# First quarter of the conv input projection summed in two halves of its contraction, its loads reordered, the norm's vector order written out, and the low parts of the expert rows made by TensorE

## Chip, cores and metric

One core of a Trainium2 chip runs one fused program. The metric is the device time of the whole program in microseconds (us), as the median of the runs shown. TensorE (PE) multiplies, VectorE (DVE) and ScalarE (ACT) work elementwise, GpSimd (POOL) does a few small steps, and SyncE (SP) issues the transfers of the weights.

## What is computed

The first block modulates a normed `x` by products of a condition vector (`ada`), runs a conformer convolution, and then a mixture of 32 experts with two chosen per token. A second block follows (latent attention and block attention), which the change does not touch.

```python
mod = silu(c) @ ada_w + ada_b                     # sh1, sc1, g1, sh2, sc2, g2
h = rmsnorm(x, norm_mix_g) * (1 + sc1) + sh1      # 256 tokens x 1024
u = h @ conv_w_in + conv_b_in;  a, gt = split(u)
u = a * sigmoid(gt)
y = depthwise_conv(u, w_dw, 31 taps) + b_dw
y = silu(layernorm(y) * ln_g + ln_b) @ conv_w_out
x = x + g1 * y
h = rmsnorm(x, norm_ffn_g) * (1 + sc2) + sh2
x = x + g2 * hier_moe(h)                          # group, top 2 of 8, 32 experts
...
```

## The kernel before, in words

**Weights.** `PIECES` lists all weights as pieces of about 2 MB. `W.fill` issues their loads on SyncE's queue in that order, each into one of six rotating buffers (later up to ten) as soon as the piece that used the buffer has been read; `W.get` hands the next one out. So the list sets the order in which weights land, and the end of the last reader of a buffer sets when a later load starts.

**Precision.** A product of the projections is made of three fp32r products: each operand is split into a high part (`wh`, `hh`, `yh`, `xh`; a ScalarE copy) and a low part (`wl`, `hl`, `yl`, `xl`; a VectorE subtraction), and high x high, low x high and high x low are summed.

**Head.** `x` is normed (`xn`) and turned (`pt`, copied to `xT`). `ada_cols` makes one 1024-vector of the modulation in two pieces: eight products `adp`, a ScalarE copy `ads`, four transposes `adc`, two short vector steps into `modc`. Vector 1 scales `xT`, vector 0 is added in `hh` (ScalarE) and `hl` (VectorE). Only when all eight 128-row chunks of `hh` and `hl` stand does the first of 16 sums `pu` begin: 24 products each, four sums for each quarter `cwi` of `conv_w_in`. The two sums of a channel group `m` are gated into `up`.

**Convolution.** VectorE runs 31 taps (L408, L411) for channel groups 0 to 3, TensorE (`pvv`, `py`) does groups 4 to 7. L479 subtracts a provisional mean.

**Norm and output.** `pms` and `pst` are column statistics, `rst` and `prs` spread the reciprocal deviation, L577 multiplies, L579 is the silu (`ysl`), and `po` multiplies by `conv_w_out`.

**Router and rows.** After the residual, VectorE runs some 35 short steps that choose the experts (up to `oh`, `pp`, `posp`), and ScalarE, GpSimd and VectorE make the scaled rows' high and low parts `xh2` and `xl2`, which the products `acc` gather for the first experts. Then 32 experts stream through `pgu` and `pys`.

A scheduler orders instructions on each engine, except where `keep_in_program_order` or a filled `pe_order` (for TensorE) holds the order of the text.

Of the kernel before, what the change touches and what calls it, by code (L numbers as in the profile page):

```python
# [13 lines left out]
P = 128  # L14
# [34 lines left out]
LN_DVE = ()  # L49
HALVED = (3,)  # L50
# [28 lines left out]
WARM_R = 2, 3  # L79
# [5 lines left out]
def pieces():  # L85
# [10 lines left out]
    add_ada(1)  # L96
    add_ada(0)
    for q in range(4):
        add((KD, 512), "cwi", 256 * q)
# [39 lines left out]
class Weights:  # L139


    def __init__(self, nc, pools, ahead):
        self.nc, self.pools, self.ahead = nc, pools, ahead
        self.src, self.tiles, self.nload, self.nget, self.cap = [], [], 0, 0, 1 << 30
        self.named, self.cuts = {}, {}
# [8 lines left out]
    def fill(self, upto):  # L154
        while self.nload < min(upto, self.cap, len(self.src)):
# [6 lines left out]
            if len(shape) == 2:  # L162
                v = v.rearrange("p (a b) -> p a b", a=shape[0])
            elif len(shape) == 3:
                v = v.rearrange("p (a b c) -> p a b c", a=shape[0], b=shape[1])
            h = n // self.cuts.get(self.nload, 1)
            for i in range(0, n, h):
                self.nc.sync.dma_start(t[:, i:i + h], ap[:, i:i + h])
            self.tiles.append(v)
# [16 lines left out]
def build(tc, A, out, dbg=None, stop=None):  # L186
# [53 lines left out]
    W.cuts = {**{i: 2 for i in HALVED}, MOE_TO - 1: LAST_CUT}  # L240
# [25 lines left out]
    crep = pre.tile([P, KD, 32], F32, name="crep")  # L266
    modc = const.tile([P, 48], F32, name="modc")
# [21 lines left out]
    def ada_part(psp, pool, ps=None):  # L289
        w = W.get()  # L290
        pt = psp.tile([P, 512], F32, name="adp", tag="adp")
        for k in range(KD):
            j = k % 4
            mm(pt[32 * j:32 * j + 32, :], crep[:, k, :], w[:, k, :], k < 4, k >= 4)
        if ps is None:
            ps = pool.tile([P, 512], F32, name="ads", tag="ads")
        nc.scalar.copy(ps, pt)
        return ps

    def ada_cols(v, psp, pool):  # L300
        for h in range(2):
            ps = ada_part(psp, pool)
            pc = psp.tile([P, 4, 4, 32], F32, name="adc", tag="adc")
            for q in range(4):
                nc.tensor.transpose(pc[:, q].rearrange("p j r -> p (j r)"), ps[:, P * q:P * q + P], ident)
            c = slice(8 * v + 4 * h, 8 * v + 4 * h + 4)
            nc.vector.reduce_sum(modc[:, c], pc[:, :, :, 0], axis=AX.X)
            nc.vector.tensor_add(modc[:, c], modc[:, c], vec[:, V_AB + 8 * v + 4 * h:V_AB + 8 * v + 4 * h + 4])
# [47 lines left out]
    def transpose_k(src, k):  # L356
        pt = psU.tile([P, T], F32, name="pt", tag="tp")
        for t in range(NT):
            nc.tensor.transpose(pt[:, P * t:P * t + P], src[:, t, P * k:P * k + P], ident)
        return pt  # L360

    ada_cols(1, psA, wk)
# [3 lines left out]
    nc.vector.scalar_tensor_tensor(aff[:, 0, :], modc[:, 8:16], 1.0, vec[:, V_MIX:V_MIX + 8],  # L366
                                   op0=OP.add, op1=OP.mult)
    for k in range(KD):
        nc.vector.tensor_scalar(xT[:, k, :], xT[:, k, :], aff[:, 0, k:k + 1], None, op0=OP.mult)
    def halves(w, c0):  # L370

        ws = []
        for i in range(2):
            wh = wsp.tile([P, 4, P], F32R, name="wh", tag="wh")
            wl = wsp.tile([P, 4, P], F32R, name="wl", tag="wl")
            split(wh, wl, w[:, 4 * i:4 * i + 4, c0:c0 + P])
            ws.append((wh, wl))
# [14 lines left out]
    def uproj(w, c0, ws=None):  # L392
        ws = ws or halves(w, c0)
# [42 lines left out]
    up = None  # L436
    for q in range(4):
        w = W.get()
        for i in range(2):
            m = 2 * q + i  # L440
            pg = uproj(w, P * i, first if m == 0 else None)
            pa = uproj(w, 256 + P * i)
            if up is None:
                up = xy.tile([P, KD, UW], F32, name="up", tag="up")
                nc.gpsimd.memset(up[:, :, 0:PADL], 0.0)
            sg = wk.tile([P, T], F32, name="sg", tag="sg")
            nc.scalar.activation(sg, pg, AF.Sigmoid, bias=vec[:, V_BIN + 8 + m:V_BIN + 9 + m])
            nc.vector.scalar_tensor_tensor(up[:, m, PADL:], pa, vec[:, V_BIN + m:V_BIN + m + 1], sg,
                                           op0=OP.add, op1=OP.mult)
    del w, first  # L450
# [67 lines left out]
    for group in CONV:  # L518
# [4 lines left out]
        for k in group:  # L523
# [27 lines left out]
    def rows_of(w, k):  # L551
# [3 lines left out]
        split(wh, wl, w[:, k, :])  # L555
        return wh, wl

    wo = W.peek(wo_at - W.nget)
    wos = [rows_of(wo, k) for k in range(WSP)]
    del wo  # L560

    nc.vector.tensor_copy(st[:, 0:4], pst)
    nc.vector.tensor_mul(st[:, 2:4], st[:, 2:4], st[:, 2:4])
    nc.vector.scalar_tensor_tensor(st[:, 0:2], st[:, 0:2], EPS, st[:, 2:4], op0=OP.add, op1=OP.subtract)
    nc.gpsimd.tensor_tensor(out=st[:, 0:2], in0=st[:, 0:2], in1=expn[:, 0:2], op=OP.pow)
    rst = wk.tile([P, T], F32, name="rst", tag="mp", bufs=1)
    for t in range(NT):
        nc.vector.tensor_scalar(rst[:, P * t:P * t + P], ident, st[:, t:t + 1], None, op0=OP.mult)
# [3 lines left out]
    for k in range(KD):  # L572
# [3 lines left out]
    for k in range(KD):  # L576
        nc.vector.tensor_mul(y[:, k, :], y[:, k, :], prs)  # L577
        ys = wk.tile([P, T], F32, name="ysl", tag="ht")
        nc.scalar.activation(ys, y[:, k, :], AF.Silu, scale=vec[:, V_LNG + k:V_LNG + k + 1],  # L579
                             bias=vec[:, V_LNB + k:V_LNB + k + 1])  # L580
        if k in LN_DVE:
            nc.vector.tensor_copy(yh[:, k, :], ys)
            nc.vector.tensor_sub(yl[:, k, :], ys, yh[:, k, :].bitcast(F32))
        else:
            split(yh[:, k, :], yl[:, k, :], ys)
# [93 lines left out]

    pw = psU.tile([P, 512], F32, name="pw", tag="pu")  # L680
    for i in range(WARM_R[0]):
        mm(pw, ident, g2b[:, 0:512], True, True)
# [1006 lines left out]
```

## Time and profile before

| | us |
|---|---|
| median of 3 runs | 946.4 (945.88 to 947.05) |
| the profiled execution | 945.95 |
| its span in the trace | 944.3 |
| TensorE busy in the span | 869.0 (92%) |
| VectorE busy | 526.6 (56%) |
| ScalarE busy | 361.2 (38%) |
| GpSimd busy | 58.2 (6%) |

The profiled execution spends 1.65 us outside the span, and lies 0.45 us under the median. The shares are averages over stages with different limits, so the rows further below are taken by stage.

### The profile page before, as it was taken

The page shows a single profiled execution, that of the slowest core. Times are in us where ns is not written, and L with a number is a line of the kernel's source. Part 1 is how long each engine was busy: PE and PEld are TensorE (multiplying, and loading weights), DVE is VectorE, ACT ScalarE, POOL GpSimd, SP SyncE. Part 2 cuts the span into 40 slices and gives each one's busy share as a digit, 9 for nine tenths or more (in the row PEclk, how much of TensorE's full clock was granted, in tenths as well). Part 3 has the DMA queues.
Part 4 walks back from the last instruction along what each step waited for, and adds up shares of the span by engine and source line. Part 5 has one row for each costly group of instructions (what it writes and reads, how often), then busy time and mean ns, then how long its engine had stood idle before and what let it go on. Part 6 is the DMA issues. An engine that isn't in the chain of part 4 may idle for free. (4 is left out here: it accounts for less than half of the span.)

```text
span 944.3 us, 15434 instructions
## 1 busy us (share of the span) xinstructions
PE 869.0 (92%) x6227; PEld 609.6 (65%) x6227; DVE 526.6 (56%) x1243; ACT 361.2 (38%) x788; POOL 58.2 (6%) x62
## 2 busy tenths in 40 slices
PE   4899879899999999999699999878999996999996
PEld 1597346665565555656356555538988874988975
DVE  2699965623343333334223342357777868758876
ACT  1455645412122121212012121145766735655761
POOL 0000210100000000000000000003100004110112
PEclk9899989999999999999899999999999998999998
DMA  9994968789999999999999999974432441624211
GB/s 372 411 389 191 406 249 317 323 362 426 427 427 428 426 427 426 427 426 430 422 428 425 426 429 425 425 311 159 170 140 91 179 178 45 255 102 179 90 45 45
DMA packets 23580, 289.44 MB, mean 307 GB/s; under 512 B 2736, under 2 KB 3408, under 8 KB 6096
## 3 DMA queue, kind: packets, MB, share of 16 engines
q1 hardware_dynamic: 21872, 282.29, 72.4%
q10 hardware_dynamic: 1632, 6.11, 1.8%
q8 instruction: 51, 0.84, 0.4%
q14 instruction: 25, 0.20, 0.1%
HBM read 287.34 MB, written 1.05 MB: 305 GB/s over the span
## 5 line engine op out<-in xcount | busy, mean ns | idle before, releaser
L197 PE MATMUL pgu<-w,xg 128*64 128x256 f32 x2048 | 233.5, 381 | 4.2 <-DMA w<-in_moe 4.2
L197 PEld LDWEIGHTS pgu<-w,xg 128*64 128x64 f32 x2048 | 145.6, 137 | 90.1 <-issue 20.8
L197 PE MATMUL pys<-w,hTe 128*64 128x512 f32 x512 | 116.1, 594 | 5.4 <-DMA w<-in_moe 2.5
L283 DVE TENSOR_TENSOR sl<-w,sh 128x1024 fp32r<-128x1024 f32 (+2 forms) x82 | 98.0, 1204 | 20.4 <-ACT sh L282 19.2
L282 ACT CAST sh<-w 128x1024 fp32r<-128x1024 f32 (+2 forms) x82 | 81.4, 1001 | 48.9 <-PE pj L197 46.0
L1012 DVE SCALAR_TENSOR_TENSOR yt<-pys,gs,g2b 64x512 f32<-64x512 f32 x64 | 48.0, 750 | 87.2 <-PE pys L197 86.2
L282 ACT CAST yh<-yt 64x512 fp32r<-64x512 f32 x64 | 39.6, 618 | 138.9 <-DVE yt L1012 137.3
L197 PE MATMUL pj<-xh,sh 128*128 128x256 f32 x304 | 86.6, 285 | 0.1
L197 PE MATMUL pj<-xl,sh 128*128 128x256 f32 x304 | 85.5, 281 | 0.0
L197 PE MATMUL pj<-xh,sl 128*128 128x256 f32 x304 | 85.3, 281 | 0.0
L197 PEld LDWEIGHTS pys<-w,hTe 128*64 128x64 f32 x512 | 36.2, 137 | 65.9 <-issue 54.5
L854 DVE TENSOR_TENSOR hid<-pgu,hid 128x256 f32<-128x256 f32 x32 | 13.6, 425 | 97.2 <-ACT hid L853 97.2
L853 ACT ACTIVATE hid<-pgu 128x256 f32<-128x256 f32 x32 | 12.3, 385 | 125.8 <-PE pgu L197 119.7
L197 PEld LDWEIGHTS pj<-xh,sh 128*128 128x128 f32 x304 | 57.1, 188 | 2.2 <-issue 1.6
L197 PEld LDWEIGHTS pj<-xl,sh 128*128 128x128 f32 x304 | 57.0, 188 | 1.8 <-issue 1.7
L197 PEld LDWEIGHTS pj<-xh,sl 128*128 128x128 f32 x304 | 57.1, 188 | 0.8 <-issue 0.8
L411 DVE SCALAR_TENSOR_TENSOR y<-up,wdw,y 128x256 f32<-128x256 f32 x120 | 54.9, 513 | 0.1
L283 DVE TENSOR_TENSOR yl<-yt,yh 64x512 fp32r<-64x512 f32 x64 | 44.0, 687 | 2.2 <-ACT yh L282 0.2
L197 PE MATMUL pu<-hh,wh 128*128 128x256 f32 x128 | 37.4, 292 | 2.7 <-ACT wh L282 2.7
L283 DVE TENSOR_TENSOR wl<-w,wh 128x512 fp32r<-128x512 f32 x48 | 33.2, 702 | 12.0 <-ACT wh L282 10.5
L282 ACT CAST wh<-w 128x512 fp32r<-128x512 f32 x48 | 29.3, 620 | 27.5 <-PE pu L197 20.4
L862 DVE COPY hTe<-pth 128x256 f32<-128x256 f32 x32 | 13.6, 425 | 44.6 <-PE pth L203 40.1
(343 smaller groups left out, 1579.2 us busy)
## 6 DMA issues: line engine op xcount, KB each, us to landing
w<-in_moe SPq DMA_DIRECT2D x95, 2048.0 KB, 32.0
w<-in_wst SPq DMA_DIRECT2D x32, 2048.0 KB, 8.7
w<-in_wst SPq DMA_DIRECT2D x5, 1152.0 KB, 5.1
w<-in_wst SPq DMA_DIRECT2D x2, 1536.0 KB, 11.2
wb<-in_wbd ACTq DMA_DIRECT2D x4, 512.0 KB, 7.0
w<-in_wst SPq DMA_DIRECT2D x2, 1024.0 KB, 22.6
w<-in_moe SPq DMA_DIRECT2D x4, 512.0 KB, 31.2
x<-in_x SPq DMA_DIRECT2D x1, 1024.0 KB, 11.5
```

The source lines that it names most:

```text
L197: ins = nc.tensor.matmul(o, l, r, start=start, stop=stop)
L282: a = nc.scalar.copy(hi, src)
L283: return a, (eng or nc.vector).tensor_sub(lo, src, hi.bitcast(F32))
L411: nc.vector.scalar_tensor_tensor(y[:, m, :], u, wdw[:, m, k:k + 1], y[:, m, :], op0=OP.mult, op1=OP.add)
L853: nc.scalar.activation(hid, pgu[:, 0:256], AF.Silu)
L854: nc.vector.tensor_mul(hid, pgu[:, 256:512], hid)
L862: nc.vector.tensor_copy(hT, pt.rearrange("p (q j s) -> p q j s", q=2, j=2))
L1012: nc.vector.scalar_tensor_tensor(yt[r, :], pys[r, :], gs[r, e % 2:e % 2 + 1], g2b[r, 512 * j:512 * j + 512], op0=OP.mult, op1=OP.mult)
```

## The change

1. **Loads.** `x` is loaded ahead of the weights. The list becomes: half 0 of modulation vectors 1 and 0, the first quarter `cwi` 0, then half 1 of vectors 1 and 0. The rows of `cwi` 0 that the second half of the sums needs (`LATE`) are loaded behind those.
2. **First quarter in halves.** Chunks 0 to 3 of `hh` and `hl` are made from the first halves of the modulation, and the four sums `pu` of the first quarter run over these chunks; chunks 4 to 7 follow. TensorE's order in the head is that of the text. Filler products `warm` (256 columns, their results unused) stand in it. Every second `xT` copy goes to ScalarE. The two sums beyond `psU`'s two buffers take `psA` tags.
3. **Norm.** ScalarE's and VectorE's order from the first `wo` splits to the last `yl` is written out; the second `adp` of the gate moves ahead of `prs`; the silu's table is loaded by an early dummy.
4. **Rows.** The low parts `xl2` of the rows are no longer made by GpSimd (row block 1) and VectorE (row block 0), but by TensorE: a product of `diag(rs2)` (`dr`) with `x2` in fp32, minus `xh2` by a negated identity, and a ScalarE copy out of PSUM. The filler products `pw` there go.

```diff
-LN_DVE = ()
-HALVED = (3,)
+LATE = {2: 4}
-WARM_R = 2, 3
+HEAD_WARM = (2, 1, 2, 1, 2)
...
-    add_ada(1)
-    add_ada(0)
-    for q in range(4):
+    for h in range(2):
+        for v in (1, 0):
+            add((KD, 512), "ada", v * D + h * 512)
+        if h == 0:
+            add((KD, 512), "cwi", 0)
+    for q in range(1, 4):
...
+            if self.nload in self.late:
+
+                self.rest[self.late[self.nload]] = t, ap
+                n //= 2
...
+    nc.sync.dma_start(x2, A["x"][0].rearrange("(t p) d -> p t d", p=P))
+    W.fill(3)
     nc.sync.dma_start(cstp, A["cst"][:, C_SEL:])
-    W.fill(1)
-    nc.sync.dma_start(x2, A["x"][0].rearrange("(t p) d -> p t d", p=P))
...
+    def ada_half(v, h, psp, pool, between=None):
+        ps = ada_part(psp, pool)
+        if between is not None:
+            between()
+        pc = psp.tile([P, 4, 4, 32], F32, name="adc", tag="adc")
+        for q in range(4):
+            tr(pc[:, q].rearrange("p j r -> p (j r)"), ps[:, P * q:P * q + P])
...
+    pe_order.append(1)
     xT = xy.tile([P, KD, T], F32, name="xT", tag="up")
     for k in range(KD):
-        nc.vector.tensor_copy(xT[:, k, :], transpose_k(xn, k))
...
+        (nc.scalar.copy if k % 2 else nc.vector.tensor_copy)(xT[:, k, :], transpose_k(xn, k))
...
+    def warm(n):
+
+        if n:
+            pw = psU.tile([P, T], F32, name="pw", tag="tp")
+            for i in range(n):
+                mm(pw, ident, x2[:, 0, 0:T], True, True)
...
+    def uproj_half(pu, i, wh, wl, between=None):
+        for k in range(4 * i, 4 * i + 4):
+            for n, (l, r) in enumerate(((wh, hh), (wh, hl), (wl, hh))):
+                mm(pu, l[:, k % 4, :], r[:, k, :], k == 0 and n == 0, k == KD - 1 and n == 2)
...
+    scale_half(0, HEAD_WARM[0])
+    shift_half(0, HEAD_WARM[1])
+    w = W.get()
+    quarter = [half(w, c0, 0) for c0 in (0, 256, P, 256 + P)]
+    warm(HEAD_WARM[2])
+    pus = [psU.tile([P, T], F32, name="pu", tag="pu") for i in range(2)]
+    pus += [psA.tile([P, T], F32, name="pu", tag=g) for g in ("adr", "pmu")]
+    for j in range(4):
+        uproj_half(pus[j], 0, *quarter[j])
+        if j == 2:
+            scale_half(1, 0)
+    warm(HEAD_WARM[3])
+    shift_half(1, HEAD_WARM[4])
+    warm(HEAD_WARM[4])
+    quarter = [half(w, c0, 1) for c0 in (0, 256, P, 256 + P)]
+    for j in range(4):
+        uproj_half(pus[j], 1, *quarter[j])
...
+    centre(0, 1, 2, 3, 4)
+    gate1.append(wk.tile([P, 512], F32, name="ads", tag="ads"))
+    keep(nc.scalar.copy(gate1[1], gate1.pop(0)))
+    keep(nc.scalar.activation(small[:, 8:9], small[:, 0:1], AF.Silu))
+    keep(nc.vector.tensor_copy(st[:, 0:4], pst))
...
+    centre(5, 6)
+    gate1.append(ada_part(psA, wk))
...
-    gate1.append(ada_part(psA, wk))
-    for k in range(KD):
-        nc.vector.tensor_sub(y[:, k, :], y[:, k, :], pms)
+    centre(7)
...
-    nc.scalar.mul(x2[:, 1, :], x2[:, 1, :], rs2[:, 1:2])
-    split(xh2[:, 1, :], xl2[:, 1, :], x2[:, 1, :], nc.gpsimd)
-    nc.scalar.activation(xh2[:, 0, :], x2[:, 0, :], AF.Identity, scale=rs2[:, 0:1])
+    def rest_of_rows(j):
+        for t in range(NT):
+            c = slice(512 * j, 512 * j + 512)
+            pw = psU.tile([P, 512], F32, name="pw", tag="pu")
+            mm(pw, dr[:, t, :], x2[:, t, c], True, False)
+            mm(pw, nident, xh2[:, t, c], False, True)
+            nc.scalar.copy(xl2[:, t, c], pw)
+
+    rest_of_rows(0)
...
-    tc.keep_in_program_order(nc.vector.scalar_tensor_tensor(
-        xl2[:, 0, :], x2[:, 0, :], rs2[:, 0:1], xh2[:, 0, :].bitcast(F32), op0=OP.mult, op1=OP.subtract))
...
+    rest_of_rows(1)
```

What this does to the engines' orders stands below, at three places. The first is TensorE in the head. Before, all transposes and the four modulation pieces come ahead of the 384 `pu` products; here are the rows of before:

```order
L197 MATMUL adp<-w,crep 32x512 x8
L305 MATMUL adc<-cst,ads 128x128 x4
L359 MATMUL pt<-cst,xn 128x128 x12
L197 MATMUL adp<-w,crep 32x512 x8
L359 MATMUL pt<-cst,xn 128x128 x4
L305 MATMUL adc<-cst,ads 128x128 x4
L197 MATMUL adp<-w,crep 32x512 x8
L305 MATMUL adc<-cst,ads 128x128 x4
L197 MATMUL adp<-w,crep 32x512 x8
L305 MATMUL adc<-cst,ads 128x128 x4
L197 MATMUL pu<-hh,wh 128x256
```

And these are the rows of the change (`pw` are the fillers; at the first mark stand 36 `pu` products, three sums over chunks 0 to 3; behind the last row the fourth sum's 12, and later the second half's 48).

```order
L212 MATMUL pt<-cst,xn 128x128 x16
L206 MATMUL adp<-w,crep 32x512 x8
L206 MATMUL pw<-x_76,cst 128x256 x2
L212 MATMUL adc<-cst,ads 128x128 x4
L206 MATMUL adp<-w,crep 32x512 x8
L206 MATMUL pw<-x_76,cst 128x256
L212 MATMUL adc<-cst,ads 128x128 x4
L206 MATMUL pw<-x_76,cst 128x256 x2
L206 MATMUL pu<-hh,wh 128x256
...
L206 MATMUL adp<-w,crep 32x512 x8
L212 MATMUL adc<-cst,ads 128x128 x4
```

What moved: half of the first quarter's products now stand ahead of the second halves of both modulation vectors on TensorE.

The second place is VectorE in the norm, behind the last tap. Before, three `wl` splits stand between the copy of the statistics (`st<-pst`) and the steps that use them:

```order
L283 TENSOR_TENSOR wl<-w,wh 128x512
L573 TENSOR_TENSOR y<-y,pms 128x256
L562 COPY st<-pst 128x4
L573 TENSOR_TENSOR y<-y,pms 128x256
L283 TENSOR_TENSOR wl<-w,wh 128x512 x3
L563 TENSOR_TENSOR st<-st 128x2
```

In the change all four splits and five centrings come first, and the statistics' steps follow one another:

```order
L295 TENSOR_TENSOR wl<-w,wh 128x512 x4
L628 TENSOR_TENSOR y<-y,pms 128x256 x5
L634 COPY st<-pst 128x4
L635 TENSOR_TENSOR st<-st 128x2
L636 SCALAR_TENSOR_TENSOR st<-st 128x2
L628 TENSOR_TENSOR y<-y,pms 128x256 x2
L642 TENSOR_SCALAR rst<-cst,st 128x128 x2
```

The splits moved ahead of the statistics, and three centrings behind them.

The third place is TensorE at the end of the same statistics. Before, the gate's second `adp` comes behind `prs`:

```order
L197 MATMUL pst<-mean_86,y 128x1 x2
L197 MATMUL pst<-mean_86,s_1385 128x1 x2
L197 MATMUL prs<-rst,ones 128x256
L197 MATMUL adp<-w,crep 32x512 x8
L197 MATMUL pl<-zeros,ones 128x72
```

In the change it comes ahead of it:

```order
L206 MATMUL pst<-mean_90,y 128x1 x2
L206 MATMUL pst<-mean_90,s_1402 128x1 x2
L206 MATMUL adp<-w,crep 32x512 x8
L206 MATMUL prs<-rst,ones 128x256
L206 MATMUL pl<-zeros,ones 128x72
```

One group of eight products changed places with `prs`.

## Rows read from the trace of the kernel before

**Rows 1.** Windows by stage: start:end, length, busy time (count) per engine, granted clock, DMA share, GB/s
```profile
0.00:36.00 36.00, 18.45 (x100) 7.09 (x100) 13.04 (x43) 9.98 (x20) 1.09 (x7) 0.98 0.95 390
36.00:84.50 48.50, 48.50 (x384) 48.28 (x385) 44.32 (x95) 21.95 (x39) 0.23 (x1) 0.95 0.83 340
84.50:122.20 37.70, 33.99 (x417) 15.93 (x415) 35.78 (x91) 23.56 (x56) 6.57 (x8) 1.00 0.85 345
122.20:138.10 15.90, 10.40 (x57) 5.37 (x57) 9.20 (x26) 6.42 (x13) 1.93 (x3) 0.79 0.47 179
...
169.50:184.30 14.80, 11.05 (x61) 7.65 (x61) 12.28 (x50) 8.60 (x18) 3.08 (x2) 1.00 0.69 273
...
193.50:620.00 426.50, 407.93 (x2949) 241.04 (x2947) 146.99 (x319) 83.72 (x170) 0.00 (x0) 0.99 1.01 426
```

**Rows 2.** Where the stream of expert weights starts: a window, and SyncE's waits, 180 to 200
```profile
190.00:193.50 3.50, 3.50 (x36) 2.31 (x34) 0.00 (x0) 0.28 (x1) 0.00 (x0) 1.00 0.35 75
...
SPq L168 <- PE pgu L197: 19.9, 2, 16.9
```

**Rows 3.** Timeline of the head: start us, us, instruction, count, [idle before <- what ended it]
```profile
11.84 3.64 PE L197 MATMUL adp<-w,crep 128*32 128x512 f32 x16 [5.98 <-DMA w<-in_wst]
14.28 1.06 ACT L350 ACTIVATE sq<-x 128x1024 f32<-128x1024 f32 x1 [7.85 <-DMA x<-in_x]
18.51 1.35 PE L359 MATMUL pt<-cst,xn 128*128 128x128 f32 x4 [0.26 <-DVE xn L354]
20.17 2.32 PE L359 MATMUL pt<-cst,xn 128*128 128x128 f32 x8 [0.30 <-DVE xT L365]
22.42 2.79 PE L197 MATMUL adp<-w,crep 128*32 128x512 f32 x16
26.52 1.92 PE L197 MATMUL adp<-w,crep 128*32 128x512 f32 x16
30.30 1.71 ACT L385 ACTIVATE hh<-xT,modc 128x256 fp32r<-128x256 f32 x4 [1.15 <-DVE modc L308]
35.91 0.58 PE L197 MATMUL pu<-hh,wh 128*128 128x256 f32 x1 [2.71 <-ACT wh L282]
```

**Rows 4.** The window of two microseconds behind the first projection product
```profile
36.00:38.00 2.00, 2.00 (x8) 1.78 (x9) 2.00 (x4) 1.42 (x3) 0.23 (x1) 0.50 0.98 368
```

**Rows 5.** VectorE's timeline: the first tap, a wait between taps
```profile
45.63 0.41 DVE L408 TENSOR_SCALAR y<-up,wdw,vec 128x256 f32<-128x256 f32 x1
...
95.83 0.43 DVE L479 TENSOR_TENSOR y<-y,mp 128x256 f32<-128x256 f32 x1 [1.67 <-ACT y L434]
```

**Rows 6.** Timeline of the norm, from the last statistics to the first output product
```profile
127.52 0.58 PE L197 MATMUL pst<-mean,s 128*128 128x1 f32 x4
128.55 1.89 DVE L283 TENSOR_TENSOR wl<-w,wh 128x512 fp32r<-128x512 f32 x3
132.37 1.19 PE L197 MATMUL prs<-rst,ones 128*128 128x256 f32 x2 [4.26 <-DVE rst L568]
133.49 3.58 PE L197 MATMUL adp<-w,crep 128*32 128x512 f32 x16
137.15 0.59 ACT L297 COPY ads<-adp 128x512 f32<-128x512 f32 x1 [1.99 <-PE adp L197]
138.09 0.49 PE L197 MATMUL po<-wh,yh 128*128 128x512 f32 x1 [0.65 <-ACT yh L282]
```

**Rows 7.** VectorE's L717 (ns min/median/max, first and last start), then the timeline around it
```profile
L717 DVE TENSOR_TENSOR t<-em,r x2: 226/1164/2101, 175.9 to 177.4; 128x64 f32<-128x64 f32 x2
...
177.09 2.38 POOL L283 TENSOR_TENSOR xl<-x,xh 128x1024 fp32r<-128x1024 f32 x1 [3.67 <-ACT xh L282]
177.97 1.88 PE L197 MATMUL pw<-g2b,cst 128*128 128x512 f32 x4
181.52 0.41 PE L197 MATMUL pp<-oh,cstp 128*128 128x32 f32 x2 [1.67 <-DVE oh L744]
184.24 0.36 PE L197 MATMUL acc<-oh,xh 128*128 128x256 f32 x1 [0.49 <-DVE oh L780]
```

More of the change, by code (lines that the diff above doesn't have):

```diff
@@ L144, in __init__ @@
         self.src, self.tiles, self.nload, self.nget, self.cap = [], [], 0, 0, 1 << 30
-        self.named, self.cuts = {}, {}
+        self.named, self.cuts, self.late, self.rest = {}, {}, {}, {}
     def add(self, ap, shape, pool=None):
@@ L239, in build @@
         W.add(src, shape, ring_a if i >= MOE_TO else None)
-    W.cuts = {**{i: 2 for i in HALVED}, MOE_TO - 1: LAST_CUT}
+    W.cuts = {MOE_TO - 1: LAST_CUT}
+    W.late = LATE
     wo_at, moe_from = WO_AT, MOE_FROM
@@ new lines, in half, with halves @@
+    def half(w, c0, i):
+        wh = wsp.tile([P, 4, P], F32R, name="wh", tag="wh")
+        wl = wsp.tile([P, 4, P], F32R, name="wl", tag="wl")
+        split(wh, wl, w[:, 4 * i:4 * i + 4, c0:c0 + P])
+        return wh, wl
+    def halves(w, c0):
+        return [half(w, c0, i) for i in range(2)]
+    y = xy.tile([P, KD, T], F32, name="y", tag="y")
+    def uproj_half(pu, i, wh, wl, between=None):
+        for k in range(4 * i, 4 * i + 4):
+            for n, (l, r) in enumerate(((wh, hh), (wh, hl), (wl, hh))):
+                mm(pu, l[:, k % 4, :], r[:, k, :], k == 0 and n == 0, k == KD - 1 and n == 2)
@@ L434, in conv_pe, with gated @@
         nc.scalar.activation(y[:, m, :], py, AF.Identity, bias=vec[:, V_BDW + m:V_BDW + m + 1])
-    up = None
-    for q in range(4):
+    def gated(m, pg, pa):
+        sg = wk.tile([P, T], F32, name="sg", tag="sg")
+        nc.scalar.activation(sg, pg, AF.Sigmoid, bias=vec[:, V_BIN + 8 + m:V_BIN + 9 + m])
+        nc.vector.scalar_tensor_tensor(up[:, m, PADL:], pa, vec[:, V_BIN + m:V_BIN + m + 1], sg,
+                                       op0=OP.add, op1=OP.mult)
+    scale_half(0, HEAD_WARM[0])
[15 more added lines that the diff above has]
+        uproj_half(pus[j], 1, *quarter[j])
+    dump("hT", hh.bitcast(F32))
+    del quarter, w
+    pe_order.clear()
+    up = xy.tile([P, KD, UW], F32, name="up", tag="up")
+    nc.gpsimd.memset(up[:, :, 0:PADL], 0.0)
+    for m in range(2):
+        gated(m, pus[2 * m], pus[2 * m + 1])
+    del pus, xT
+    for q in range(1, 4):
         w = W.get()
         for i in range(2):
[L440 to L450, printed above, removed]
+            gated(2 * q + i, uproj(w, P * i), uproj(w, 256 + P * i))
+    del w
     dump("u", up)
@@ L575, in build @@
     yl = xt.tile([P, KD, T], F32R, name="yl")
[L576 to L585, printed above, removed]
+    yss = []
@@ new lines, in build @@
+    for k in range(KD + 1):
+        if k < KD:
+            keep(nc.vector.tensor_mul(y[:, k, :], y[:, k, :], prs))
+            yss.append(wk.tile([P, T], F32, name="ysl", tag="ht"))
+            keep(nc.scalar.activation(yss[k], y[:, k, :], AF.Silu, scale=vec[:, V_LNG + k:V_LNG + k + 1],
+                                      bias=vec[:, V_LNB + k:V_LNB + k + 1]))
+        if k:
+            keep(nc.scalar.copy(yh[:, k - 1, :], yss[k - 1]))
+            keep(nc.vector.tensor_sub(yl[:, k - 1, :], yss[k - 1], yh[:, k - 1, :].bitcast(F32)))
@@ L588, in build @@
+    del yss
     x2T = y
@@ L751, in build @@
     nc.vector.scalar_tensor_tensor(posp, pp, 1.0, oh1, op0=OP.add, op1=OP.mult)
-    for i in range(WARM_R[1]):
-        mm(pw[:, 0:256], ident, g2b[:, 0:256], True, True)
-    del pw
+    rest_of_rows(1)
     dump("posp", posp)
```

91 lines of the change are left out of this document (48 added, 43 removed).

## The prediction

> **What bounds the kernel now.** I read the windows by stage first [rows 1]. From 193.5 to 620 us the DMA engines are full (share 1.01, 426 GB/s) and TensorE is busy 407.9 of 426.5 us: the experts' weights stream in, and nothing in the change makes that stream shorter. What starts it is in the next view: between 190 and 193.5 us the DMA share is 0.35, and SyncE's queue waits for `pgu` products, 19.9 us in all [rows 2]. The buffers are full, and the stream goes on when TensorE has read the first expert's weights. So the time by which the work ahead of the experts gets shorter should come off the whole. That work has four stages with different limits [rows 1]: to 36 us TensorE is busy for half of the time and waits; from 36 to 84.5 us it has no gap; from 84.5 to 122.2 us VectorE is the fuller one (35.8 of 37.7 us); from 122.2 to 138.1 us no engine is busy for more than 10.4 of 15.9 us, so this is a chain of waits; from 169.5 to 184.3 us VectorE (12.3) and TensorE (11.1) take turns. The sum below is made against the profiled execution, 945.95 us, of which 944.3 is span; the median lies 0.45 us above it.
>
> **Loads and norm of `x`.** Before, the first weights landed at 11.8 and `x` at about 14.2 us (`adp` and the squares start on them) [rows 3]. A 2 MB piece takes 2.1 MB / 426 GB/s = 4.9 us [rows 1]. With `x` ahead it lands near 14.2 - 4.9 - 0.4 (a small constant that moves behind) = 8.9 us, the modulation pieces at 13.8 and 18.8, half of `cwi` 0 at 21.3, the other two pieces at 26.5 and 31.5, and the rest of `cwi` 0 at 33.9. All these are estimates from the two landings. From `x` to the first transpose took 18.5 - 14.2 = 4.3 us [rows 3], so 13.2 now. Sixteen transposes at 2.32 / 8 = 0.29 us [rows 3]: 17.8.
>
> **TensorE in the head.** One `adp` group took 3.64 us at the slow clock, 2.79 while the clock rose and 1.92 at the fast one [rows 3]. I take 3.1 for the first: its end is 20.9. Its copy, transposes and one filler pair follow, and the second group starts near 22.0. From a group's start to the first `hh` were 30.30 - 26.52 = 3.8 us [rows 3]; so `hh` starts near 25.8. Then 36 products; at 48.5 / 384 = 0.126 us [rows 1] they are 4.5 us, but they start on one `hh` and `hl` after the other (1.71 for four) and on splits behind them, so I take until 31.3. The third group, its copy and its transposes then hold the queue: 3.1 us, 34.4; the fourth sum and a filler 1.9; the last group starts at 36.3 and its `hh` at 40.1. VectorE's order puts two splits (1.89 / 3 = 0.63 each [rows 6]) ahead of the last four `hl`, so the first sum of the second half ends near 43 and the 48 products near 47.4. Before, the same 96 products ended near 50 (84.5 less 288 products at 0.12). TensorE gains 2.5 us. The fillers lie in the 0.6 us of each copy and cost what they exceed it; without them the cost would be the clock, below.
>
> **VectorE behind it.** The first tap came at 45.6 [rows 5]. It needs two finished sums, 44.6 now, and the gating, so 45.1; but until about 50.8 VectorE then does two splits and one gating more and four taps fewer than before, which cancels the lead. So the taps gain nothing (bounds: 1.5 earlier, 1.5 later). They don't have to. At 95.83 VectorE had waited 1.67 us for `y` of a group that TensorE and ScalarE make [rows 5]. With TensorE 2.5 us ahead that wait goes, and behind it VectorE is full until 122: the gain is **1.7 us** (bounds 0.2 and 3.2).
>
> **The norm.** Three pieces. The statistics are complete on TensorE at 127.5 + 0.6 = 128.1, and then 1.89 us of splits stand before the steps that use them; `prs` starts at 132.4 [rows 6]. In the new order splits and centrings fill VectorE's time up to the statistics, and these come 0.8 us earlier since part of `adp` no longer lies between them; I put `prs` at 130.1, 2.25 us earlier. `prs` itself took 1.19 us at the slow clock, 0.6 at the fast: 0.6. Behind it ScalarE made two silus, then waited 1.99 us for the gate's `adp` (3.58 us, slow clock), then copied, and only then made `yh` for the first `po` at 138.1 [rows 6]. Now `adp` runs while TensorE would wait for `rst` (4.26 us of wait cover its 1.92 to 3.6), ScalarE's copy is done before, and one silu and one copy lead to `po`: 2.6 us less. Together 5.4. Against it stands the clock: TensorE still has a gap ahead of `po`, and where the grant falls to 1.2 GHz in it, the first `po` products take twice as long for some 3 us. I take off 0.8: **4.6 us** (bounds 3 and 5.5). Behind it the `po` stage is TensorE's, and unchanged.
>
> **The rows.** GpSimd's subtraction ran from 177.09 for 2.38 us, and a small step of VectorE on the route, which had taken 0.23 us at 175.9, took 2.10 from 177.4 on, inside it [rows 7]. Without it `oh` and `pp` could start 1.9 us earlier, at 179.6. But TensorE now makes the low parts. An fp32 pass of 512 columns is about 0.43 us (four in 1.88 [rows 7]), two passes for `dr`; the fp32r product is one pass at 2 x 0.126 = 0.25 us. A row block and half is 1.1 us, four of them 4.4, of which 1.9 were filler time before. From 178.0, two of them end at 180.2; `pp` takes 0.7; two more end at 183.1; `acc` follows there instead of at 184.2. Its ScalarE copies lie behind the products, and the last is needed only by the gather's second half. The gain is **1.1 us** (bounds: 0.3, if ScalarE's copies hold a PSUM buffer, and 1.9, if only the route counts).
>
> **Sum.** 1.7 + 4.6 + 1.1 = 7.4 us: 945.95 - 7.4 = 938.5 for the profiled execution, 939.0 for the median.
>
> **A rule that speaks against the head.** Row: before, the `adp` group at 22.4 us began slow and ended fast, behind 12 transposes that kept TensorE busy from 18.5 [rows 3]. The Trainium skill, TensorE: Matmul & The Clock Gate, section "Part 4: PE-mode transpose", says that transposes don't count as TensorE activity for the clock gate. The row doesn't decide it, since the rise came inside the product that followed them. By the row's mixed price the sum is as above.
>
> **Rivals.**
> - *The clock stays slow longer.* The 16 transposes leave the grant at 1.2 GHz: the first `adp` takes 3.64 us, its fillers 0.9 more, TensorE gains only 1.1 and the taps come 1.4 later: the wait at 95.83 shrinks by 0.3. In the norm the clock costs 1.6 instead of 0.8. Then 0.3 + 3.8 + 1.1 = 5.2 us: 941.2. For it: before, the grant was 0.50 in the first projection products, behind a stretch of waits [rows 4]. Against: the new head has fewer waits. The skill's rule above would give this case in the head.
> - *Everything falls well.* The first `adp` is fast and `po` too: 3.0 + 5.4 + 1.5 = 9.9 us: 936.5.
> - *The gain is given back to the weights.* If the stream from 193.5 us on were set by its bytes alone, the earlier start of the experts would only be waited off, and the time would be 946.4. Against: the queue stands at 190 us because buffers are full [rows 2], and it would start earlier too.
> - *Slower.* One mechanism: the second half of the first quarter starts late because its modulation sums stand on TensorE behind the first half's products. If the clock falls to 1.2 GHz between them, products, sums and fillers from 31 us on (about 14 us at the fast clock) double; the first tap then comes at 59, VectorE is 13 us late less the 1.7 of its wait, and the end is 11.6 - 5.7 = 6 us later: 952. It decides from 7.4 us of lateness of the first tap on. Against: the fillers stand just there.
>
> **Numbers.** My forecast has 0.52, the slow clock 0.20, the good case 0.15, the weights 0.07, slower 0.06. The likeliest gives 939.0, with a range of its own of 937.3 to 940.8. The range of 8 in 10 takes in the first two rivals: 935.2 to 942.6. Within 0.2% (1.9 us, about what a measurement of this kernel tells from no change) lie the fourth case and hardly any other: faster 0.87, same 0.07, slower 0.06.
>
> **What would show it.** In the new trace: `x`'s squares near 9 us; the 96th `pu` product near 47.4; no wait of VectorE of over 0.5 us between taps; the first tap near 45; `prs` 5 to 8 us behind the last tap and `po` 2 to 3 us behind `prs`, with ScalarE's gate copy ahead of the silus; no row of about 2 us on the route; `acc` near 176.8, and the DMA stream 7 us earlier. The prediction is wrong if the first tap is after 47, if the granted clock falls below 1.00 in 30 to 47 us, or if `acc` is early and the end isn't.

## The result, and the profile after

The changed kernel took 950.91 us, the median of 5 runs (950.07 to 953.27), against 945.88 us of the kernel before beside it (944.60 to 947.05): a ratio of 1.0057, with an interval of 1.0040 to 1.0075. It is slower by 5 us, where the prediction had 7.4 us less. The profiled execution took 950.07 us, 948.1 of it span (before 945.95 and 944.3).

The windows by stage of the changed kernel, with the columns of [rows 1]:

```profile
0.00:36.00 36.00, 22.74 (x141) 13.47 (x145) 12.43 (x38) 10.81 (x21) 1.01 (x6) 1.00 0.95 393
...
122.20:138.10 15.90, 12.73 (x50) 8.88 (x50) 6.97 (x20) 4.74 (x9) 4.31 (x3) 0.57 0.41 142
...
193.50:620.00 426.50, 408.52 (x2969) 242.28 (x2965) 146.95 (x319) 84.78 (x171) 0.00 (x0) 0.99 1.00 423
```

The head does more than before in the same time: 22.74 us of TensorE instead of 18.45. The view gives 1.00 as its granted clock. This can't be taken for the first microseconds: the first `adp` took 2.36 us where the higher clock takes 1.92, so it began slow, and the first one of before was slow throughout (3.64 us [rows 3]) in a stage for which the view gives 0.98. From 30 to 47 us the granted clock is 1.00. The weights' stream is as full as it was. The stage that stands out is the fourth: the granted clock was 0.79 there and is 0.57, so TensorE is busy longer (12.73 instead of 10.40 us) with fewer products.

The timeline of the changed kernel, head first, then the tail of the convolution on VectorE:

```profile
7.92 1.06 ACT L370 ACTIVATE sq<-x 128x1024 f32<-128x1024 f32 x1 [1.43 <-DMA x<-in_x]
17.26 2.36 PE L206 MATMUL adp<-w,crep 128*32 128x512 f32 x16
...
46.96 0.28 PE L206 MATMUL pu<-hh,wl 128*128 128x256 f32 x1
...
93.51 0.76 DVE L538 TENSOR_TENSOR y<-y,mp 128x256 f32<-128x256 f32 x2 [1.90 <-ACT y L471]
121.71 1.09 DVE L538 TENSOR_TENSOR y<-y,mp 128x256 f32<-128x256 f32 x3
122.72 1.89 DVE L295 TENSOR_TENSOR wl<-w,wh 128x512 fp32r<-128x512 f32 x3
```

The pace of the head is the predicted one: `x` is there at 7.9, the first tap starts at 45.03, the 96th `pu` product (the row of 46.96) about 3 us before its place in the kernel before. But VectorE still waits between taps: 1.90 us at 93.5 where there were 1.67 at 95.8 [rows 5]. It came to that place sooner, with 52 taps left behind it where 47 were left before (counted in both timelines), and a second wait for a `y` of ScalarE, 0.50 us at 112.88, is new. So its last tap ends at 121.79, 0.65 us later than before (121.14).

The norm, in the kernel before:

```profile
120.36 1.64 PE L197 MATMUL adp<-w,crep 128*32 128x512 f32 x7
121.62 1.11 POOL L471 TENSOR_TENSOR asum<-asum,y 128x256 f32<-128x256 f32 x1 [4.72 <-DVE y L479]
122.79 0.70 PE L197 MATMUL pms<-asum,mean 128*128 128x256 f32 x2 [0.79 <-POOL asum L471]
124.29 1.06 PE L197 MATMUL adp<-w,crep 128*32 128x512 f32 x6
```

and in the changed kernel:

```profile
118.46 1.88 PE L206 MATMUL adp<-w,crep 128*32 128x512 f32 x13
122.27 2.92 POOL L530 TENSOR_TENSOR asum<-asum,y 128x256 f32<-128x256 f32 x1 [7.10 <-DVE y L538]
125.24 1.22 PE L206 MATMUL pms<-asum,mean 128*128 128x256 f32 x2 [4.90 <-POOL asum L530]
132.09 0.99 PE L206 MATMUL pst<-mean,s 128*128 128x1 f32 x4
133.01 3.64 PE L206 MATMUL adp<-w,crep 128*32 128x512 f32 x16
136.58 1.22 PE L206 MATMUL prs<-rst,ones 128*128 128x256 f32 x2
```

TensorE ends the gate's first `adp` at 120.3, waits 4.90 us for GpSimd's sum `asum`, and then runs the statistics, the second `adp` and `prs` at the lower clock: each `pms` takes 1.20 us instead of 0.70, and `adp` 3.64 where the higher clock takes 1.92 [rows 3]. In the kernel before the wait was 0.79 us and the statistics ran at the higher clock; `prs` and the second `adp` were slow there too [rows 6].

The output stage and the rows, as windows (from the first `po` to the router's `rs`, and from there to the first expert product), of the kernel before:

```profile
138.09:173.45 35.36, 34.23 (x181) 24.55 (x181) 19.19 (x39) 18.66 (x41) 0.70 (x1) 1.00 0.76 298
173.45:188.31 14.86, 12.02 (x71) 8.79 (x70) 11.78 (x48) 7.08 (x14) 2.38 (x1) 1.00 0.93 376
```

and of the changed one:

```profile
139.73:176.63 36.90, 35.78 (x180) 25.53 (x181) 21.48 (x44) 18.94 (x40) 0.70 (x1) 0.95 0.67 269
176.63:192.06 15.43, 13.52 (x73) 9.28 (x72) 8.92 (x47) 8.71 (x19) 0.00 (x0) 1.00 0.92 356
```

Both stages are longer; in the first the clock is lower, in the second it is not. The end of the route, in the timeline of the changed kernel, with a new wait of 2.04 us behind the products `pw`:

```profile
183.52 0.41 PE L206 MATMUL pp<-oh,cstp 128*128 128x32 f32 x2
186.68 1.07 DVE L857 TENSOR_SCALAR oh<-cst,posp 128x64 fp32r<-128x64 f32 x6 [2.04 <-PE pw L206]
187.57 0.36 PE L206 MATMUL acc<-oh,xh 128*128 128x256 f32 x1 [0.93 <-DVE oh L857]
```

The differences add up, after minus before: last tap +0.65; from it to the first `pms` +1.80 (3.45 instead of 1.65); from there to the end of the last `pst` +2.53 (7.84 instead of 5.31); to `prs` -0.77; to the first `po` -2.57; the output stage +1.54; the rows +0.57. That is +3.75 at the first expert product, and +3.8 at the end of the span. Beside the forecast: the taps +0.65 where 1.7 less was forecast; the norm with its clock +2.53 (0.99 up to the first `po`, 1.54 in the output stage) where 4.6 less was; the rows +0.57 where 1.1 less was. The medians differ by 5.0; the other 1.2 us is within what executions of one kernel differ by (last section).

### The profile page after: what moved, and what is told of

Read it like the earlier page. It is cut to its first block, busy times and chain, and to the rows that moved or that the text cites. A ratio compares the mean times of both kernels' runs of the same rounds, so it can differ in the third digit from the quotient of the medians.

```text
span 948.1 us, 15477 instructions
## 1 busy us (share of the span) xinstructions
PE 877.6 (93%) x6249; PEld 617.5 (65%) x6249; DVE 522.3 (55%) x1240; ACT 363.8 (38%) x798; POOL 57.7 (6%) x61
## 5 line engine op out<-in xcount | busy, mean ns | idle before, releaser
L206 PE MATMUL pu<-hl,wh 128*128 128x256 f32 x128 | 36.4, 284 | 0.8 <-DVE hl L409 0.7
```

The costliest lines, as they stand in the source:

```text
L206: ins = nc.tensor.matmul(o, l, r, start=start, stop=stop)
```

## The experiments

First theory: the new norm does the damage, since its splits run beside GpSimd's sum, TensorE waits, and its clock falls. The first four kernels take the change apart: the head (loads and first quarter) alone, the norm alone, the rows alone, and the head with the rows. Their diffs are the parts 1 and 2, 3, and 4 of the change.

**Head alone (head_only).**

> The loads and the first quarter in halves alone; norm and rows as before. Theory N (the loss is the norm's): the 96th pu product near 47 us, the last tap at about 121.7 (0.6 later than before, since VectorE's order puts 52 taps behind the wait at 93.5 where before 47 stood behind it), TensorE's wait for asum 0.8 to 1.5 us with asum near 1.1 us, and 945.9 to 947.0 in all. Theory H (the head starts the loss, through the later last subtractions): prs at 134 or later and over 948.5.

Measured: 948.96 us, ratio 1.0033 (1.0019 to 1.0047). TensorE's rows in the norm:

```profile
122.25 1.71 POOL L532 TENSOR_TENSOR asum<-asum,y 128x256 f32<-128x256 f32 x1 [7.10 <-DVE y L540]
124.01 1.22 PE L208 MATMUL pms<-asum,mean 128*128 128x256 f32 x2 [3.69 <-POOL asum L532]
135.50 1.19 PE L208 MATMUL prs<-rst,ones 128*128 128x256 f32 x2 [3.65 <-DVE rst L629]
136.62 3.64 PE L208 MATMUL adp<-w,crep 128*32 128x512 f32 x16
```

The old norm, and yet the wait (3.69), the slow `pms` and `adp`, and a `prs` 3.1 us later than before. So the first theory falls: the head alone is enough.

**Norm alone (norm_only).**

> The norm's written order alone; head and rows as before. Theory N: asum takes 2.5 to 3 us beside VectorE's splits (1.11 before), TensorE waits over 4 us for it, the granted clock in the statistics is 0.50, prs starts 3 to 4 us later than 132.4, and the whole is 2.5 to 3.5 us slower: 948.4 to 949.4. Theory H (only the later last subtractions of the head bring it about): prs no later than before and 942 to 944. Rival R (the parts are harmless alone): within 1 us of 945.9.

Measured: 943.95 us, ratio 0.9967 (0.9953 to 0.9981). The norm alone is faster by 0.3%:

```profile
120.28 1.11 POOL L474 TENSOR_TENSOR asum<-asum,y 128x256 f32<-128x256 f32 x1 [4.72 <-DVE y L482]
121.45 0.70 PE L197 MATMUL pms<-asum,mean 128*128 128x256 f32 x2 [0.99 <-POOL asum L474]
```

and its output stage as a window:

```profile
132.67:169.75 37.08, 35.95 (x180) 25.50 (x181) 21.44 (x44) 18.96 (x40) 0.70 (x1) 0.95 0.65 266
```

TensorE's first `adp` reaches into the statistics as before, the wait is 0.99 us, the statistics fast. No split runs beside the sum `asum` here: the first starts at 121.52, behind its copy `wh` on ScalarE. From the last tap's end to the first `po` are 12.87 us, where the kernel before has 16.95: 4.1 us less. But the output stage takes 37.08 us, 1.7 more than before, at a granted clock of 0.95.

**Rows alone (rows_only).**

> The low parts of the rows by products alone; head and norm as before. If the rows by products cost: pp 1.2 us nearer to the end of the output stage, but acc 0.1 and the first pgu 0.5 us further from it, 946.0 to 946.8. If the gain of the sum on record holds: 944.8. If they are the loss: over 949.

Measured: 946.39 us, ratio 0.9992 (0.9978 to 1.0006), no difference. From `rs` to `pp` it took 6.90 us (8.07 before), from `pp` to `acc` 4.04 (2.72 before), to the first expert product 4.39 (4.07): the route is shorter by what the products behind it take.

**Head and rows (head_rows).**

> The changed kernel with the norm of before: head and rows. Theory N: 946.0 to 947.5, so that giving back the norm alone wins back 3 to 5 us of 950.9. Theory H: 949.5 or more.

Measured: 951.05 us, ratio 1.0048 (1.0031 to 1.0065); taking the new norm out wins nothing. What theory H said holds as far as the head starts the loss. How it does so is the next question: by TensorE's idle time and its clock (T), by the sum that GpSimd makes beside VectorE (C), or by VectorE's order itself (L).

**Fillers in the wait (fill).** TensorE's products of the last statistics are put behind the fillers in its order.

```diff
                     gate1 = [ada_sums(psA, W.get())]
+                    warm(10)
```

> The changed kernel with ten filler products of 256 columns on TensorE between the gate's first adp and the statistics, where it had waited 4.90 us for asum; the statistics' own order as in the changed kernel. Theory T (TensorE runs ahead of VectorE, idles, and its clock falls): asum still 2.9 us, pms still near 125.2, but the granted clock 1.00 in the statistics, prs near 131.6 instead of 136.6, po near 134.2, 945.5 to 947. Rival C (the wait itself is the loss, through GpSimd beside VectorE's splits): no gain from the fillers, 950 to 951.5.

Measured: 947.67 us, ratio 1.0022 (1.0005 to 1.0038), 3.2 us under the changed kernel.

```profile
123.59 2.92 POOL L530 TENSOR_TENSOR asum<-asum,y 128x256 f32<-128x256 f32 x1 [7.10 <-DVE y L538]
126.55 0.70 PE L206 MATMUL pms<-asum,mean 128*128 128x256 f32 x2 [0.38 <-POOL asum L530]
133.60 0.67 PE L206 MATMUL prs<-rst,ones 128*128 128x256 f32 x2 [1.06 <-DVE rst L653]
```

`asum` is as long and `pms` no sooner (its head came 1.3 us later in this execution), but all products are fast, and from `pms` to `prs` are 7.05 us instead of 11.34. Useless work on TensorE wins 4.3 us here.

**Splits behind the sums (probe).**

```diff
+    keep(nc.vector.tensor_copy(small[:, 9:10], ssum[:, 0:1]))
     wos = [rows_of(wo, k, True) for k in range(WSP)]
```

> The changed kernel with one short VectorE copy of a column of ssum ahead of the splits wl in VectorE's order, so that the splits begin when GpSimd's sums are done. Theory T: asum 1.1 us instead of 2.92, pms near 123.4, but TensorE has still been idle for 3 us and the clock is 0.50: prs near 134.8, 949 to 949.6. Rival C: with the short asum the gap is short enough and the norm is whole: 945 to 946.

Measured: 947.26 us, ratio 1.0021 (1.0004 to 1.0038).

```profile
122.61 1.11 POOL L530 TENSOR_TENSOR asum<-asum,y 128x256 f32<-128x256 f32 x1 [7.10 <-DVE y L538]
123.78 0.97 PE L206 MATMUL pms<-asum,mean 128*128 128x256 f32 x2 [3.09 <-POOL asum L530]
```

The sum takes 1.11 us when no split runs beside it: the 1.8 us are that contention. The rest of the statistics stays slow (0.85 and 1.20 a row), so there are two prices. Neither theory's range was met: by the median this run gains as much as the ten fillers do (947.26 and 947.67). Part of it is that the clock rises inside the second `adp` (3.39 us), so that `prs` takes 0.70 us instead of 1.22; which price is the larger in the changed kernel the medians don't say.

**Second `adp` in the wait (early_probe).** As the run before, and

```diff
-                    gate1 = [ada_sums(psA, W.get())]
+                    gate1 = [ada_part(psA, wk)]
+                    gate1.append(ada_part(psA, wk))
...
     centre(5, 6)
-    gate1.append(ada_part(psA, wk))
```

> The copy as in the run on contention, and the gate's second adp moved ahead of the statistics, into TensorE's wait for asum, instead of ahead of prs. Theory T: TensorE is busy to about 122.9, waits 0.5 us, clock 1.00 in the statistics, prs near 129.3 and po near 132: 943 to 944.5. Rival C: as the run on contention, less the 1.6 us that adp held prs back: 944 to 947.

Measured: 943.53 us, ratio 0.9986 (0.9976 to 0.9996): 7.4 us under the changed kernel.

```profile
121.52 1.92 PE L206 MATMUL adp<-w,crep 128*32 128x512 f32 x16 [0.68 <-ACT ads L312]
123.94 0.70 PE L206 MATMUL pms<-asum,mean 128*128 128x256 f32 x2 [0.50 <-POOL asum L530]
130.99 1.19 PE L206 MATMUL prs<-rst,ones 128*128 128x256 f32 x2 [2.91 <-DVE rst L651]
```

and the output stage as a window:

```profile
134.11:171.26 37.15, 36.03 (x181) 25.99 (x181) 21.43 (x44) 18.84 (x40) 0.70 (x1) 0.94 0.57 228
```

The statistics are fast, and `adp` does useful work where the fillers stood. But now TensorE waits 2.91 us ahead of `prs`, `prs` is slow, and the output stage begins at the lower clock: 37.15 us again.

**And fillers ahead of `po` (all).** `pms` products first, then

```diff
     mm(prs, ones, rst, True, True)
+    warm(4)
```

> As the run before it, with the three pms products ahead of all pst products, so that the centring starts sooner, and four filler products between prs and po. Theory T: prs near 129, no granted clock under 1.00 between 125 and 145, so the output stage takes 1 to 1.5 us less too: 941.5 to 943.5, and so under the kernel before by 3 to 4 us. Rival C: no better than the run before it.

Measured: 946.60 us, ratio 1.0012 (0.9998 to 1.0026): the forecast of T for the whole is missed. In the trace the stages did what T said (the output stage, and the rows behind it, as windows):

```profile
134.63:169.76 35.13, 34.01 (x183) 24.54 (x182) 20.59 (x42) 18.72 (x40) 0.70 (x1) 1.00 0.60 240
169.76:185.07 15.31, 13.40 (x72) 9.16 (x71) 8.88 (x47) 8.71 (x19) 0.00 (x0) 1.00 0.92 355
```

The clock is 1.00, the stage 2.0 us shorter, the first expert product starts at 185.07, 3.2 us sooner than before. The profiled execution was one of the shortest of twelve (944.1 to 950.7), so it shows only a part of where the median lost that. The last section comes back to it.

**The head with fillers (head_fill).** The head alone, old norm, old rows, and eight fillers behind the first `adp`.

> The kernel with the head alone, which was 2.6 us slower than the kernel before, with eight filler products between the gate's first adp and the statistics; norm and rows of before. Theory T (the whole loss of the head is TensorE's idle time ahead of the statistics and the clock behind it): clock 1.00 in the statistics, prs near 133.5 instead of 135.5, the second adp in 1.92 instead of 3.64 us, po near 137.5 instead of 141.3, 945.0 to 946.3. Rival L (the head loses through VectorE's later last subtractions): 948 to 949.

Measured: 945.36 us, ratio 0.9995 (0.9982 to 1.0008).

```profile
120.18 3.72 PE L208 MATMUL pw<-x,cst 128*128 128x256 f32 x16
122.18 1.71 POOL L532 TENSOR_TENSOR asum<-asum,y 128x256 f32<-128x256 f32 x1 [7.10 <-DVE y L540]
123.94 0.70 PE L208 MATMUL pms<-asum,mean 128*128 128x256 f32 x2
130.53 1.00 PE L208 MATMUL prs<-rst,ones 128*128 128x256 f32 x2 [2.45 <-DVE rst L640]
```

`asum` and the start of `pms` are those of the head alone (1.71 us; 123.94 and 124.01), VectorE's last subtractions too, and the order of TensorE's statistics. Only the idle time is filled, and `prs` starts 5.0 us sooner and the first `po` 5.6. The median is 3.6 us less than without fillers: the loss of the head is gone, though nothing is gained on the kernel before. This settles T against C and L for the head.

**Later subtractions (late).** As early_probe; the two subtractions of 93.5 are held behind the 15th tap of the last two groups.

```diff
+                if then is not None and len(ms) * k + ms.index(m) + 1 == at:
+                    tc.keep_in_program_order(tap)
+                    then()
```

> As early_probe, and VectorE's two subtractions that wait for y at 93.5 stand five taps later, 47 taps from the end as in the kernel before instead of 52. Theory O (the order gave the head's lead away): the wait of 1.90 us falls under 0.3, the last tap ends 1.6 to 2.1 us nearer to the first one (76.8 us from the first tap's start to the last one's end in the changed kernel, then 74.7 to 75.2), and the time is 1 to 2 us under early_probe: 941.5 to 942.5. Rival: another wait between taps takes its place, and the last tap moves by under 0.5 us.

Measured: 946.68 us, ratio 0.9991 (0.9975 to 1.0008). VectorE's waits of over half a microsecond between taps:

```profile
96.11 0.17 DVE L323 TENSOR_REDUCE modc<-adc 128x4 f32<-128x16 f32 x1 [1.52 <-PE adc L212]
102.64 0.42 DVE L541 TENSOR_TENSOR y<-y,mp 128x256 f32<-128x256 f32 x1 [0.55 <-ACT y L474]
```

The rival is right: another wait for TensorE takes the place, and first tap to last tap takes 76.42 us instead of 76.76.

**All of it (best).** The kernel called all, with the later subtractions.

> As the kernel called all, with the same later subtractions. Theories T and O: first expert product 3 to 5 us earlier than before, 941 to 943.5 in all.

Measured: 948.13 us, ratio 1.0015 (1.0000 to 1.0030). Missed. In its trace the first `po` and `rs` come as hoped (135.32, 170.50), but the rows stage, unchanged, was slow:

```profile
170.50:190.13 19.63, 17.74 (x77) 12.51 (x76) 8.90 (x47) 8.82 (x19) 0.00 (x0) 0.77 0.77 302
```

**Norm alone, `adp` behind `prs` (norm_late).**

```diff
-    gate1.append(ada_part(psA, wk))
...
     mm(prs, ones, rst, True, True)
+    gate2 = ada_sums(psA, W.get())
...
+        if k == 1:
+            gate1.append(wk.tile([P, 512], F32, name="ads", tag="ads"))
+            keep(nc.scalar.copy(gate1[1], gate2))
```

> The kernel with the norm alone (old head, old rows), but with the gate's second adp behind prs, where TensorE otherwise waits for the first yh, and ScalarE's copy of it behind the first yh. Theory T: prs 0.8 us earlier, adp in 1.92 us at a granted clock of 1.00, no clock of 0.50 in the first po products, 1 to 2 us under the kernel with the norm alone: 941.5 to 943. Rival: the copy holds ScalarE up and po starves, 944 to 945.

Measured: 943.86 us, ratio 0.9979 (0.9966 to 0.9992).

```profile
130.08 1.19 PE L197 MATMUL prs<-rst,ones 128*128 128x256 f32 x2 [2.04 <-DVE rst L585]
131.20 2.96 PE L197 MATMUL adp<-w,crep 128*32 128x512 f32 x16
```

and the output stage as a window:

```profile
134.34:169.68 35.34, 34.22 (x182) 24.46 (x182) 20.62 (x42) 19.47 (x41) 0.70 (x1) 1.00 0.76 298
```

`adp` itself was not fast (2.96), and the first `po` comes 0.4 us later behind the last tap than in the norm alone (13.27 and 12.87); but the clock has risen when `po` starts, and the output stage is 1.7 us shorter than there. Its first expert product is the earliest of all, 184.53. By the median it is level with the norm alone; these two and early_probe are the versions that beat both kernels. Of the three only early_probe has the new head, and it is not ahead of the others.

Side by side, times in us, all but the median from the traces. The kernel before beside the four groups of runs had 945.88 (after), 946.35 (the first four), 945.67 (fill to all) and 946.23 (the rest), so the ratios above compare better than the medians. A trace is one execution: that of head_only took 951.89 us and that of head_fill 943.36, so what sets the two apart is read from the stages and the medians, and not from the ends of the two traces.

| kernel | median | first tap | last tap's end | pms | prs | first po | first pgu |
|---|---|---|---|---|---|---|---|
| before | 945.88 | 45.63 | 121.14 | 122.79 | 132.37 | 138.09 | 188.31 |
| after | 950.91 | 45.03 | 121.79 | 125.24 | 136.58 | 139.73 | 192.06 |
| head_only | 948.96 | 45.01 | 121.77 | 124.01 | 135.50 | 141.28 | 191.58 |
| head_fill | 945.36 | 44.94 | 121.69 | 123.94 | 130.53 | 135.71 | 186.01 |
| norm_only | 943.95 | 44.28 | 119.80 | 121.45 | 129.52 | 132.67 | 185.31 |
| norm_late | 943.86 | 45.56 | 121.07 | 122.72 | 130.08 | 134.34 | 184.53 |
| head_rows | 951.05 | 44.46 | 121.21 | 123.46 | 134.95 | 140.72 | 191.40 |
| rows_only | 946.39 | 45.73 | 121.34 | 122.98 | 132.56 | 137.69 | 188.39 |
| fill | 947.67 | 46.35 | 123.11 | 126.55 | 133.60 | 136.20 | 188.40 |
| probe | 947.26 | 45.38 | 122.14 | 123.78 | 134.62 | 137.25 | 189.53 |
| early_probe | 943.53 | 45.52 | 122.29 | 123.94 | 130.99 | 134.11 | 186.57 |
| all | 946.60 | 45.08 | 121.82 | 123.47 | 130.47 | 134.63 | 185.07 |
| late | 946.68 | 46.44 | 122.86 | 124.54 | 131.59 | 134.71 | 187.73 |
| best | 948.13 | 45.52 | 121.96 | 123.64 | 130.64 | 135.32 | 190.13 |

## Why the prediction was wrong, by its steps

**The head: right up to VectorE, wrong behind it.** `x`'s squares, the first tap and the 96th product came within 1.1 us of the forecast. The step that failed first is "With TensorE 2.5 us ahead that wait goes, and behind it VectorE is full until 122". TensorE was ahead, but VectorE's order had moved too: the waiting subtractions stand five taps sooner in it, so the wait went along. Instead of 1.7 us less, the last tap ended 0.65 us later: VectorE went on 2.3 us sooner behind the wait, with five more taps to do and the new wait of 0.50 us. Held back by hand, the subtractions only made room for a wait for `adc` (late). What the order of VectorE shows at that place, 52 taps behind it and not 47, was to be read before any run.

**The norm: the missing step.** A lead that VectorE doesn't take up becomes idle time of TensorE. The prediction asked what the earlier TensorE would do to VectorE's wait, and not what TensorE does itself when it has finished the gate's `adp` sooner (120.3 instead of 122.0, the ends before the two waits) and the sum it needs comes no sooner. In the kernel before, `adp` reached to 122.0 and a last piece of it into the statistics and was the cover; the change moved it away. The clock was priced at 0.8 us and only "ahead of `po`". It cost, in the statistics, 7.84 us where the same products without the piece of `adp` (1.06) took 4.25 before: 3.6 us. head_only against head_fill shows this by itself: 3.6 us in the median.

**The norm: other terms.** "In the new order splits and centrings fill VectorE's time up to the statistics" left out that GpSimd makes the last sum just then: 2.92 us with the splits beside it, 1.11 without (probe), 1.8 us on the path. `prs`, put at 0.6 us, took 1.22 at the lower clock. And `adp` ahead of `prs`, costed at nothing because of a wait of 4.26 us, ran at the lower clock and held `prs` until 136.58, 1.5 us after `rst` was made (134.65 and 0.48).

**The norm: what held.** ScalarE's copy out of the way was to bring 2.6 us between `prs` and the first `po`: it brought 2.57. With its cover in place, the norm alone is 4.1 us shorter from last tap to first `po`, where the forecast had 5.4 ahead of the clock's 0.8; its output stage is 1.7 us longer, so 2.4 of 4.6 us are left, as much as its median gained. What was not seen is that the `adp` taken from between `prs` and `po` had kept TensorE at work there: without it some of the first products of the output stage run at the lower clock, and the stage takes 36.9 to 37.7 us (six kernels) instead of 35.1 to 35.4 in those that have fillers or `adp` there. So "behind it the `po` stage is TensorE's, and unchanged" was wrong by 1.5 us.

**The rows.** The route got shorter, by 1.18 us from `rs` to `pp`, and the 2 us row is gone. But "`acc` follows there" left out that VectorE's rows `oh` for the gather wait for the last `pw` product (2.04 us), and `acc` for them (0.93). So +1.33 from `pp` to `acc`, 0.42 more from there to the first expert product, and +0.57 for the stage where 1.1 us of gain stood. Why `oh` waits for `pw` was not tried. In the kernel's text the memory of `dr`, an operand of these products, is given back right behind them and that of `oh` is taken right after, so the two may be the same memory; this is not shown.

**The rivals.** The slow clock was one of them, with its price in the head (where it did not fall: 1.00 from 30 to 47 us) and 1.6 us in the norm. The place was wrong and the size less than half. Behind 16 transposes the first `adp` took 2.36 us: the first four of its 16 rows took 0.86 us, as in the slow group at 133.01, and the next four 0.47. So the clock rose inside this group, as it did inside the second `adp` of before [rows 3]. The rule on transposes that the prediction cites from the Trainium skill (TensorE: Matmul & The Clock Gate, section "Part 4: PE-mode transpose") is neither shown nor refuted by that; the 3.64 us did not come. The rival "slower" had its mechanism in the head, and was wrong too. That the weights take the gain back did not happen either: from the first expert product to the end of the last one (`pys`) all 14 traces take 436.5 to 437.0 us, whether the first came at 184.53 or at 192.06.

## What to carry to other kernels

When an engine is made faster up to a point where it waits for another, look for what it will do in the new wait. If it is TensorE, the products behind the wait may run at half the rate, and the lead is paid back with interest; fill the wait with work that must be done anyway, and move nothing away that fills one now. And read the engine's order on both sides of a wait before calling it gone: the instruction that waits may have moved with the lead.

## What the runs showed of the hardware

**TensorE's clock behind a wait.** The same two-pass product `prs` took 0.67 us behind a wait of 1.06 us (fill), 1.00 behind 2.45 (head_fill), 1.19 behind 2.04, 2.91 and 3.65 (norm_late, early_probe, head_only). The rows before it differ, so the wait alone does not set it. The granted clock in these rows is one of two levels, 1.2 and 2.4 GHz; this the Trainium skill says too (TensorE: Matmul & The Clock Gate, section "Part 1: The HAM clock gate (the "warmup" mystery)"): a gate that grants half or all of the rate by how busy TensorE has been. The trace agrees; the experiments with fillers show that work whose result nobody uses is as good as any.

**GpSimd beside VectorE.** GpSimd's addition of 128 x 256 took 0.71 us where VectorE ran nothing beside it (`ssum` in probe). The last `asum` took 1.11 us with the end of VectorE's three subtractions of `mp` beside it, 1.71 where one split follows these without a gap (head_only), and 2.92 where three do. TensorE, which needs it, started 0.05 to 0.06 us after its end each time. The Trainium skill (SBUF — State Buffer, section "SBUF: two separate sides") says that the two engines share a port pair, which whoever starts first holds for the whole instruction while the other waits; on VectorE this is said of operations with two SBUF inputs, among others. The rows agree. In the changed kernel VectorE is in a subtraction (from 122.05) when the addition begins (122.27); subtractions and splits then follow one another without a gap until 124.60, and the addition ends at 125.19. In head_only VectorE leaves a gap of 0.12 us behind the first split: the addition ends at 123.95, and it is the second split that takes longer, 1.02 us instead of 0.68. In the kernel before `ssum` began first and kept its 0.73 us, and the split that met it took 1.10:

```profile
122.69 0.73 POOL L484 TENSOR_TENSOR ssum<-ssum,s 128x256 f32<-128x256 f32 x1
122.86 1.10 DVE L283 TENSOR_TENSOR wl<-w,wh 128x512 fp32r<-128x512 f32 x1 [0.72 <-ACT wh L282]
```

So a row of GpSimd or VectorE can hold a wait for the other engine, and gaps between VectorE's rows decide when GpSimd gets its turn.

**One stage, two clocks.** The rows stage of the kernels called all and best holds the same instructions; in one execution it took 15.31 us at a granted clock of 1.00, in the other 19.63 at 0.77. Executions of one kernel lay up to 6.7 us apart (late, 942.6 to 949.3). A single trace shows where a stage's time goes, but a gain of 2 us counts only when a median of ten shows it. For the kernel called all it did not. A part of the loss lies behind the experts, in the second block, whose text no run changed: it took 317.4 to 322.0 us in the 14 traces of the table. The four longest (all, norm_only, late, head_only: 321.0 to 322.0) are those with a granted clock of 0.83 from 160 to 200 us into the block, where the others have 0.87 to 0.91. Here is that stretch in the kernel before (a block of 319.4 us) and in the kernel called all (321.0 us), as windows:

```profile
784.90:824.90 40.00, 32.31 (x211) 28.60 (x212) 31.93 (x45) 22.85 (x45) 13.12 (x9) 0.91 0.40 150
781.82:821.82 40.00, 32.14 (x193) 27.62 (x194) 30.61 (x44) 22.58 (x46) 12.38 (x8) 0.83 0.37 130
```

So of the 3.2 us by which the trace of all is ahead at the first expert product, 1.7 were lost there. Where its other executions lost the rest stays open; the rows stage and the second block are two places where such a loss was seen.
